# A gated delta net's key-key and query-key products: plain float32 against three terms of exactly split operands

## The chip, the cores and the metric

The kernel runs on one core of a Trainium2 chip. The metric is the device time of one execution in microseconds (us), the median of several runs. Durations inside an execution come from one profiled run of the program.

## The reference, cut to what matters

One layer of a decoder trunk: 512 tokens, a model width of 2048, all in float32. After a norm and one input projection, three groups of heads work side by side: six heads of stick-breaking attention, four groups of a short gated convolution, and six heads of a gated delta net. Their outputs go through an output projection and a squared-ReLU MLP. The change lies in the delta net, of which this is the part that counts:

```python
def gated_delta_rule(q, k, v, g, beta):      # chunks of C tokens, H heads, head width 128
    ...
    k_beta = k * beta[..., None]
    m = jnp.where(strict, jnp.einsum('bhnid,bhnjd->bhnij', k_beta, k) * decay, 0.0)
    t_mat = lax.linalg.triangular_solve(eye + m, ..., lower=True, unit_diagonal=True)
    u = t_mat @ v_beta
    w = t_mat @ (k_beta * jnp.exp(g)[..., None])
    attn_intra = jnp.where(tri, jnp.einsum('bhnid,bhnjd->bhnij', q, k) * decay, 0.0)
    ...
    def step(state, xs):
        v_new = u_c - w_c @ state
        o = q_c @ state + a_c @ v_new
        state = state * jnp.exp(gl_c)[..., None, None] + jnp.swapaxes(k_c, -1, -2) @ v_new
        return state, o
```

`k` and `q` come from the projection through a causal convolution of four taps, a SiLU and an l2 norm. Within a chunk, the products of all keys with all keys (for `m`) and with all queries (for `attn_intra`) are formed, weighted by a decay and masked; a triangular system is solved; then the chunks follow one another through a state.

## The kernel before

Tokens lie along the free dimension (512 columns) and channels along the 128 partitions. The kernel takes chunks of 128 tokens instead of 64, so a head has four blocks (`NB = 4`).

A float32 product can be formed in two ways on TensorE. A matmul with plain float32 operands is one call in the code. Or each operand is split into a high part of type `float32r` and the remainder, also of that type; then three matmuls (high by high, high by low, low by high) are added up in PSUM. The helper `mm3` does this, with one line for each term (L116, L117, L118). The projections (`gemm`, `gemm_chunk`) and the MLP work in this way: ScalarE casts the weights to the high part (`whi`, L103; in the MLP `W`, L841) and VectorE subtracts to get the low part (`wlo`, L104; in the MLP L842). The delta net's own small matmuls are plain float32.

The delta net runs in these steps for each head `h`:

- `gdn_in(h)`: three projections of 48 matmuls x 512 columns (key, query, value; the first head's are computed with the start of the kernel), each through `conv_silu`; `l2n` for key and query. The normalised key and query are written by VectorE into the tile `kq` (L372 and L374), laid out as [128, block, key or query, 128]. Then the value is transposed (L380), the decay matrix is built (L386 to L398: the matmuls are L389), and for each block one matmul takes the key as the stationary operand and key and query together, 256 columns, as the moving operand (L404). VectorE multiplies the two halves of the result with the masked decay into `MT` (L406) and `AT` (L407). PSUM tiles with the tag `i` (two banks) serve the transposition, the decay, the l2 norm and these products in turn.
- `gdn_base(h)`: the triangular inverse, from `MT`. It moves 32x32 blocks through DRAM, runs 31 short steps on VectorE and some small matmuls (L463 to L493).
- `gdn_kdec(h)` and `gdn_scan(h)`: the four blocks in order, each with three to four small matmuls that depend on one another (L507, L512, L517, L526, L530), and at the end a transposition (L544).
- `gdn_gate(h)`: one more projection, the gate.

The calls are written out by hand: `gdn_in(0)`, `base(0)`, `gdn_in(1)`, `scan(0)`, a group of the short convolution, `base(1)`, `gdn_in(2)`, and so on. The order on each engine isn't that of the program text: the framework's planner works out an order for every engine ahead of time from its own costs and from priorities. `base` and `scan` are given a high priority (`CPRIO`), weight loads a medium one (`WPRIO`); `gdn_in` has none. So projections, which need nothing but weights, are placed between the steps of the scans. At run time each engine works through its own order, with semaphores between engines. After the delta net, its SBUF pool (`gdn`) and PSUM pools are closed, and the attention stage opens its own in the same place (`sq`, `sk` and others), starting with the scores (PSUM tag `z`). Then come the output projection and the MLP, which hold most of the time.

Of the kernel before, what the change touches and what calls it, by code (L numbers as in the profile page):

```python
# [11 lines left out]
F32 = mybir.dt.float32  # L12
F32R = mybir.dt.float32r
AF = mybir.ActivationFunctionType
ALU = mybir.AluOpType

P = 128
T = 512
NB = T // P
# [35 lines left out]
def trunk(ctx, tc, xT, wv1, wv2, wa, wo, wu, wd, vec, wf, out, dbg=None):  # L55
    nc = tc.nc
    V, S, G, PE = nc.vector, nc.scalar, nc.gpsimd, nc.tensor
# [19 lines left out]
    def xps(tag):  # L77
        pool, bufs = pool_of[tag]
        return pool.tile([P, 512], F32, name=tag, tag=tag, bufs=bufs)
# [34 lines left out]
    def mm3(p, lh, ll, rh, rl, first, last, more=False):  # L114

        PE.matmul(p, lhsT=lh, rhs=rh, start=first, stop=False, skip_group_check=more)  # L116
        PE.matmul(p, lhsT=lh, rhs=rl, start=False, stop=False, skip_group_check=more)  # L117
        return PE.matmul(p, lhsT=ll, rhs=rh, start=False, stop=last, skip_group_check=more)  # L118
# [10 lines left out]
    def gemm(src, acts):  # L129
        p = mmps()  # L130
        for c in range(KT // CHUNK_KT):
            gemm_chunk(p, src, acts, c)
        return p

    def silu(x, s):

        S.activation(out=s, in_=x, func=AF.Abs)
        S.activation(out=s, in_=s, func=AF.Exp, scale=-1.0)
        S.activation(out=s, in_=s, func=AF.Ln, bias=1.0)
        V.scalar_tensor_tensor(out=s, in0=x, scalar=0.0, in1=s, op0=ALU.min, op1=ALU.subtract)  # L140
        S.activation(out=s, in_=s, func=AF.Exp)
        V.tensor_tensor(out=x, in0=x, in1=s, op=ALU.mult)
# [20 lines left out]
    def col(c):  # L163
        return vc[:, c:c + 1]
# [121 lines left out]
    def ytile(i):  # L286
        return y_pool.tile([P, 512], F32, name="y", tag=f"y{i}", bufs=(10, 6)[i])
# [48 lines left out]
    def gt(shape, name, tag=None, bufs=1, dt=F32):  # L336
        return gp.tile(shape, dt, name=name, tag=tag or name, bufs=bufs)
# [3 lines left out]
    def conv_silu(p, ti):  # L341
        xp = gt([P, 516], "xp", bufs=1)
        G.memset(xp[:, 0:3], 0.0)
        V.tensor_tensor(out=xp[:, 3:515], in0=p, in1=R, op=ALU.mult)
        cv = gt([P, 512], "cv", bufs=2)
        w = lambda i: col(C_GCW + ti * 4 + i)
        S.activation(out=cv, in_=xp[:, 3:515], func=AF.Copy, scale=w(3))
        for i in (2, 1, 0):
            V.scalar_tensor_tensor(out=cv, in0=xp[:, i:i + 512], scalar=w(i), in1=cv, op0=ALU.mult, op1=ALU.add)
        silu(cv, gt([P, 512], "sg", bufs=1))  # L350
        return cv

    def l2n(cv, bias):
        sq = gt([P, 512], "g", tag="g", bufs=4)
        S.activation(out=sq, in_=cv, func=AF.Square)
        hl = [gt([P, 512], "g", tag="g", bufs=4, dt=F32R) for _ in range(2)]
        S.copy(out=hl[0], in_=sq)
        V.tensor_tensor(out=hl[1], in0=sq, in1=hl[0].bitcast(F32), op=ALU.subtract)
        p = xps("i")
        for i in range(2):  # L360
            PE.matmul(p, lhsT=onesR, rhs=hl[i], start=i == 0, stop=i == 1)
        rsqrt_exp(sq, p, 1.0, bias)
        return q4(cv), q4(sq)
# [3 lines left out]
    def gdn_in(h):  # L367
        st = {}
        prod = lambda i: first[i] if h == 0 else gemm(wa[3 * h + i], xw)
        c, r = l2n(conv_silu(prod(0), NH + h), None)  # L370
        kq = gt([P, NB, 2, P], "kq", bufs=3)
        V.tensor_tensor(out=kq[:, :, 0], in0=c, in1=r, op=ALU.mult)  # L372
        c, r = l2n(conv_silu(prod(1), h), lns_c)
        V.tensor_tensor(out=kq[:, :, 1], in0=c, in1=r, op=ALU.mult)  # L374
        cv = conv_silu(prod(2), 2 * NH + h)

        vtok = ytile(1)
        p = xps("i")
        for b in range(NB):
            PE.transpose(p[:, b * P:(b + 1) * P], cv[:, b * P:(b + 1) * P], ident)  # L380
        S.copy(out=vtok, in_=p)

        G1 = [gt([P, NB, P], "g", tag="g", bufs=4, dt=F32R) for i in range(2)]
        for i in range(2):
            for b in range(NB):
                S.activation(out=G1[i][:, b], in_=U32, func=AF.Copy, scale=ghl[:, i, b, h:h + 1].bitcast(F32))  # L386
        p = xps("i")
        for i in range(2):
            PE.matmul(p, lhsT=SLR, rhs=G1[i].rearrange("p b f -> p (b f)"), start=i == 0, stop=i == 1)  # L389
        dti = gt([P, 512], "g", tag="g", bufs=4)  # L390
        dts = gt([P, 512], "g", tag="g", bufs=4)
        S.activation(out=dti, in_=p, func=AF.Exp)
        G.affine_select(out=q4(dts), in_=q4(dti), compare_op=ALU.is_gt, fill=0.0, base=0,
                        pattern=[[0, NB], [1, P]], channel_multiplier=-1)
        G.affine_select(out=q4(dti), in_=q4(dti), compare_op=ALU.is_ge, fill=0.0, base=0,
                        pattern=[[0, NB], [1, P]], channel_multiplier=-1)
        for b in range(NB):
            S.activation(out=q4(dts)[:, b], in_=q4(dts)[:, b], func=AF.Copy, scale=be[:, b, h:h + 1])  # L398
        AT, MT = ytile(1), gt([P, 512], "MT", bufs=3)
        for c in range(2):  # L400
            p = xps("i")
            pv = p.rearrange("p (b w f) -> p b w f", b=2, w=2)
            for b in range(2):
                PE.matmul(pv[:, b], lhsT=kq[:, 2 * c + b, 0], rhs=kq[:, 2 * c + b], start=True, stop=True)  # L404
            s = slice(2 * c, 2 * c + 2)
            V.tensor_tensor(out=q4(MT)[:, s], in0=pv[:, :, 0], in1=q4(dts)[:, s], op=ALU.mult)  # L406
            V.tensor_tensor(out=q4(AT)[:, s], in0=pv[:, :, 1], in1=q4(dti)[:, s], op=ALU.mult)  # L407
        st.update(kq=kq, vtok=vtok, AT=AT, MT=MT)
        heads[h] = st
# [250 lines left out]
    def scan(h):  # L660
        with tc.high_priority(CPRIO):
            gdn_kdec(h)
            gdn_scan(h)

    gdn_in(0)
    base(0)
    gdn_in(1)
    scan(0)
    sc_group(0)
    base(1)  # L670
    gdn_in(2)
    scan(1)
    gdn_gate(0)
# [576 lines left out]
```

## Time and profile before

| what | value |
|---|---|
| runs | 2169.36, 2166.35, 2168.53 us; median 2168.53 |
| the profiled execution | 2170.97 us |
| its span, first to last instruction | 2169.3 us |
| mean granted TensorE clock | 0.996 |
| TensorE matmul (PE) busy | 2140.7 us, 12674 matmuls |
| VectorE (DVE) busy | 1660.4 us |
| ScalarE (ACT) busy | 1073.7 us |
| matmuls of L404 | 48 records |

How to read it: the span is the time between the first and the last instruction in the trace, and the execution's own time is 1.7 us longer. PE is the matmul itself, PEld the load of its stationary operand, which is an instruction of its own. Matmuls are pipelined, so one record can begin before the one ahead of it ends: what a matmul costs is the time from its start to the next one's start, not its recorded duration. Rows of groups read: line, engine, operation, output <- inputs, shapes, count | busy us, mean ns of one | idle time of that engine just before, and what ended it.

### The profile page before, as it was taken

The page shows a single profiled execution, that of the slowest core. Times are in us where ns is not written, and L with a number is a line of the kernel's source. Part 1 is how long each engine was busy: PE and PEld are TensorE (multiplying, and loading weights), DVE is VectorE, ACT ScalarE, POOL GpSimd, SP SyncE. Part 2 cuts the span into 40 slices and gives each one's busy share as a digit, 9 for nine tenths or more (in the row PEclk, how much of TensorE's full clock was granted, in tenths as well). Part 3 has the DMA queues.
Part 4 walks back from the last instruction along what each step waited for, and adds up shares of the span by engine and source line. Part 5 has one row for each costly group of instructions (what it writes and reads, how often), then busy time and mean ns, then how long its engine had stood idle before and what let it go on. Part 6 is the DMA issues. An engine that isn't in the chain of part 4 may idle for free.

```text
span 2169.3 us, 33100 instructions
## 1 busy us (share of the span) xinstructions
PE 2140.7 (99%) x12674; PEld 1884.5 (87%) x12674; DVE 1660.4 (77%) x2360; ACT 1073.7 (49%) x1629; POOL 131.8 (6%) x188
## 2 busy tenths in 40 slices
PE   9999999999999999899999999999999999999998
PEld 8887888888988888799999999999878888888886
DVE  6678978644657755477888788778898898898897
ACT  5646666333445544444444454445544444454455
POOL 0000000000000011100000000000001000000101
PEclk9999999999999999899999999999999999999999
DMA  6333232322222354666666665666896877787674
GB/s 184 107 99 95 82 91 91 92 92 84 83 83 83 103 169 150 215 188 196 194 174 187 195 192 172 191 195 181 280 310 182 242 219 196 208 228 226 184 213 117
DMA packets 160719, 356.42 MB, mean 164 GB/s; under 512 B 20273, under 2 KB 62257, under 8 KB 160433
## 3 DMA queue, kind: packets, MB, share of 16 engines
q1 hardware_dynamic: 146304, 302.93, 41.4%
q0 software_dynamic: 13968, 50.86, 13.6%
q8 instruction: 99, 1.62, 0.3%
q14 instruction: 60, 0.48, 0.1%
q10 hardware_dynamic: 288, 0.52, 0.1%
HBM read 308.90 MB, written 45.36 MB: 163 GB/s over the span
## 4 chain that ended last, share of the span: by engine, by line
PE 92%; DVE 3%; DMA 2%; ACT 1%; issue 1%; SPq 0%; DVEq 0%; ACTq 0%
PE mm L117 10%; PE mm L116 10%; PE mm L118 10%; PE pu L118 10%; PE pu L116 10%; PE pu L117 10%; PE pp L117 9%; PE pp L118 9%; PE pp L116 9%; PE mm L280 1%; PE mm L281 1%; PE mm L279 1%; DMA ha<-hs 1%; DVE W L842 1%; DMA q<-in_wu_dram 0%
## 5 line engine op out<-in xcount | busy, mean ns | idle before, releaser
L841 ACT CAST W<-q 128x1024 fp32r<-128x1024 f32 x446 | 466.7, 1054 | 579.4 <-PE pp L118 258.0
L842 DVE TENSOR_TENSOR W<-q,W 128x1024 fp32r<-128x1024 f32 x446 | 540.9, 1221 | 134.8 <-ACT W L841 130.7
L116 PE MATMUL mm<-big,whi 128*128 128x512 f32 x1024 | 404.8, 396 | 1.3 <-ACT whi L103 0.6
L117 PE MATMUL mm<-big,whi 128*128 128x512 f32 x1024 | 403.9, 394 | 0.0
L118 PE MATMUL mm<-big,wlo 128*128 128x512 f32 x1024 | 402.5, 393 | 0.0
L117 PE MATMUL pp<-W,A 128*128 128x512 f32 x888 | 346.1, 390 | 1.0 <-DVE W L842 1.0
L118 PE MATMUL pp<-W,A 128*128 128x512 f32 x888 | 345.7, 389 | 0.4 <-DVE A L842 0.4
L116 PE MATMUL pp<-W,A 128*128 128x512 f32 x888 | 343.3, 389 | 1.4 <-ACT W L841 1.1
L104 DVE TENSOR_TENSOR wlo<-raw,whi 128x512 fp32r<-128x512 f32 (+1 forms) x292 | 196.6, 675 | 158.3 <-ACT whi L103 150.4
L103 ACT CAST whi<-raw 128x512 fp32r<-128x512 f32 (+1 forms) x292 | 177.3, 608 | 276.5 <-PE mm L117 239.0
L116 PE MATMUL pu<-XS,W 128*128 128x256 f32 x1024 | 288.4, 282 | 9.8 <-ACT W L841 9.6
L118 PE MATMUL pu<-XS,W 128*128 128x256 f32 x1024 | 287.7, 281 | 0.5 <-DVE W L842 0.5
L117 PE MATMUL pu<-XS,W 128*128 128x256 f32 x1024 | 287.8, 281 | 0.0
L116 PEld LDWEIGHTS mm<-big,whi 128*128 128x128 f32 x1024 | 192.4, 188 | 41.4 <-ACT whi L103 2.0
L118 PEld LDWEIGHTS mm<-big,wlo 128*128 128x128 f32 x1024 | 192.4, 188 | 39.1 <-DVE wlo L104 0.3
L117 PEld LDWEIGHTS mm<-big,whi 128*128 128x128 f32 x1024 | 192.5, 188 | 39.0 <-DVE big L734 0.3
L116 PEld LDWEIGHTS pu<-XS,W 128*128 128x128 f32 x1024 | 193.8, 189 | 10.8 <-ACT W L841 9.8
L116 PEld LDWEIGHTS pp<-W,A 128*128 128x128 f32 x888 | 166.7, 188 | 37.1 <-ACT W L841 2.5
L117 PEld LDWEIGHTS pp<-W,A 128*128 128x128 f32 x888 | 166.7, 188 | 37.0 <-DVE W L842 2.5
L118 PEld LDWEIGHTS pp<-W,A 128*128 128x128 f32 x888 | 166.7, 188 | 35.3 <-DVE A L842 0.8
L859 DVE TENSOR_TENSOR q<-q 128x1024 f32<-128x1024 f32 x159 | 193.9, 1220 | 2.2 <-DMA q<-in_wd_dram 0.9
L118 PEld LDWEIGHTS pu<-XS,W 128*128 128x128 f32 x1024 | 193.7, 189 | 0.8 <-DVE W L842 0.8
(302 smaller groups left out, 3284.9 us busy)
## 6 DMA issues: line engine op xcount, KB each, us to landing
q<-in_wu_dram SPq DMA_DIRECT2D x128, 512.0 KB, 4.9
q<-in_wd_dram SPq DMA_DIRECT2D x128, 512.0 KB, 5.6
raw<-in_wa_dram SPq DMA_DIRECT2D x192, 256.0 KB, 2.9
hs<-h SPq DMA_DIRECT2D x32, 1024.0 KB, 5.3
q<-in_wd_dram POOLq DMA_DIRECT2D x64, 512.0 KB, 6.9
ha<-hs SPq DMA_DIRECT2D x55, 512.0 KB, 6.6
q<-in_wu_dram POOLq DMA_DIRECT2D x33, 512.0 KB, 5.6
raw<-in_wo_dram SPq DMA_DIRECT2D x64, 256.0 KB, 3.0
```

What stands on the lines that cost most here:

```text
L103: S.copy(out=hi[:, :n], in_=raw[:, :n])
L104: V.tensor_tensor(out=lo[:, :n], in0=raw[:, :n], in1=hi[:, :n].bitcast(F32), op=ALU.subtract)
L116: PE.matmul(p, lhsT=lh, rhs=rh, start=first, stop=False, skip_group_check=more)
L117: PE.matmul(p, lhsT=lh, rhs=rl, start=False, stop=False, skip_group_check=more)
L118: return PE.matmul(p, lhsT=ll, rhs=rh, start=False, stop=last, skip_group_check=more)
L279: PE.matmul(o, lhsT=xw[k][:, 0, s], rhs=hi[:, ws], start=k == 0 and b % 2 == 0, stop=False)
L280: PE.matmul(o, lhsT=xw[k][:, 0, s], rhs=lo[:, ws], start=False, stop=False)
L281: PE.matmul(o, lhsT=xw[k][:, 1, s], rhs=hi[:, ws], start=False, stop=k == KT - 1 and b % 2 == 1)
L841: return (S.copy(out=o[:, 0], in_=src), V.tensor_tensor(out=o[:, 1], in0=src, in1=o[:, 0].bitcast(F32), op=ALU.subtract))
L842: V.tensor_tensor(out=o[:, 1], in0=src, in1=o[:, 0].bitcast(F32), op=ALU.subtract))
L859: on_v = lambda t, u: V.tensor_tensor(out=t, in0=t, in1=u, op=ALU.add)
```

## The change

In `gdn_in`, the tile `kq` is split into a high and a low part in a new tile `kqs` (one buffer), by a cast on ScalarE and a subtraction on VectorE, each over the whole of the head's keys and queries (128 x 1024). The four products of the head use `mm3` on these parts, three `float32r` matmuls of 256 columns each, instead of one plain float32 matmul. `kq` itself stays, for the scans. All else is left as it was.

```diff
@@ -372,6 +372,9 @@
         V.tensor_tensor(out=kq[:, :, 0], in0=c, in1=r, op=ALU.mult)
         c, r = l2n(conv_silu(prod(1), h), lns_c)
         V.tensor_tensor(out=kq[:, :, 1], in0=c, in1=r, op=ALU.mult)
+        kqs = gt([P, 2, NB, 2, P], "kqs", dt=F32R)
+        S.copy(out=kqs[:, 0], in_=kq)
+        V.tensor_tensor(out=kqs[:, 1], in0=kq, in1=kqs[:, 0].bitcast(F32), op=ALU.subtract)
         cv = conv_silu(prod(2), 2 * NH + h)
 
         vtok = ytile(1)
@@ -400,8 +403,8 @@
         for c in range(2):
             p = xps("i")
             pv = p.rearrange("p (b w f) -> p b w f", b=2, w=2)
-            for b in range(2):
-                PE.matmul(pv[:, b], lhsT=kq[:, 2 * c + b, 0], rhs=kq[:, 2 * c + b], start=True, stop=True)
+            for b in (2 * c, 2 * c + 1):
+                mm3(pv[:, b % 2], kqs[:, 0, b, 0], kqs[:, 1, b, 0], kqs[:, 0, b], kqs[:, 1, b], True, True)
             s = slice(2 * c, 2 * c + 2)
             V.tensor_tensor(out=q4(MT)[:, s], in0=pv[:, :, 0], in1=q4(dts)[:, s], op=ALU.mult)
             V.tensor_tensor(out=q4(AT)[:, s], in0=pv[:, :, 1], in1=q4(dti)[:, s], op=ALU.mult)
```

## The prediction, made before the changed kernel was run

> **What bounds the kernel now.** I read the page's totals and chain first, then the sums by stage, then PE's waits, then the rows of the changed lines. The page:
>
> ```profile
> span 2169.3 us, 33100 instructions
> ...
> PE 2140.7 (99%) x12674; PEld 1884.5 (87%) x12674; DVE 1660.4 (77%) x2360; ACT 1073.7 (49%) x1629; POOL 131.8 (6%) x188
> ...
> PE 92%; DVE 3%; DMA 2%; ACT 1%; issue 1%; SPq 0%; DVEq 0%; ACTq 0%
> ```
>
> PE carries 92% of the chain that ended last, so in most stages a microsecond of matmul saved is a microsecond of kernel. A busy share of 99% alone would not say so, because matmul records overlap. The changed products and the scans that use them lie between about 90 and 530 us. The sums by stage there (busy us of PE, PEld, DVE, ACT, POOL, then clock, DMA share, GB/s):
>
> ```profile
> 60.00:140.00 80.00, 78.99 (x358) 64.73 (x357) 57.24 (x115) 54.05 (x114) 3.43 (x10) 1.00 0.32 98
> 140.00:220.00 80.00, 79.88 (x425) 63.79 (x424) 63.88 (x184) 42.67 (x89) 3.70 (x10) 1.00 0.34 98
> 220.00:300.00 80.00, 80.00 (x428) 65.35 (x427) 70.80 (x190) 53.86 (x112) 2.23 (x7) 1.00 0.29 89
> 300.00:380.00 80.00, 80.00 (x434) 65.31 (x433) 62.95 (x167) 48.89 (x105) 3.19 (x9) 1.00 0.29 87
> ```
>
> PE has next to no idle time there (at most 1.0 of 80 us), at a granted clock of 1.00. VectorE is the next engine (70.80 of 80 us at its fullest), ScalarE has a third or more free. PE's waits from 60 to 560 us (total, times, longest):
>
> ```profile
> PE r L226 <- ACT R L146: 0.8, 1, 0.8
> PE z L116 <- ACT sk L582: 0.4, 1, 0.4
> PE mm L116 <- ACT sq L585: 0.4, 1, 0.4
> PE mm L116 <- DVE xp L344: 0.2, 1, 0.2
> ```
>
> None is in the delta net's own work: its latencies are covered by projection matmuls (mm) that stand between its steps in PE's order. The feed of those projections runs ahead:
>
> ```profile
> L103 ACT CAST whi<-raw 128x512 fp32r<-128x512 f32 x152 | 94.0, 619 | 129.3 <-PE mm L117 115.8 <-PE mm L281 6.4 <-DVE Yq L449 2.4
> ```
>
> ScalarE's idle time ahead of the weight casts was ended by PE in 115.8 of 129.3 us: the casts wait for PE to free a buffer, not PE for the casts.
>
> **The change part by part.** *The products.* Each head has four products (one for each block of 128 tokens) of 256 columns, six heads 24. Their rows now:
>
> ```profile
> L404 PEld LDWEIGHTS i<-kq x48: 186/189/192, 111.5 to 378.5; 128*128 128x128 f32 x48
> L404 PE MATMUL i<-kq x48: 377/379/483, 111.7 to 378.7; 128*128 128x256 f32 x48
> L507 PE MATMUL s<-Sn,kq x36: 270/275/377, 198.9 to 508.1; 128*128 128x128 f32 x36
> L372 DVE TENSOR_TENSOR kq<-cv,g x6: 680/685/694, 90.1 to 354.7; 128x512 f32<-128x512 f32 x6
> L374 DVE TENSOR_TENSOR kq<-cv,g x6: 682/685/689, 96.6 to 355.3; 128x512 f32<-128x512 f32 x6
> ```
>
> 48 matmuls for 24 products: a plain float32 product is issued as two passes. The recorded 379 ns is a latency; what a pass costs is start to start. The first head:
>
> ```profile
> 111.45 0.40 PE L118 MATMUL mm<-big,wlo 128*128 128x512 f32 x1
> 111.68 1.02 PE L404 MATMUL i<-kq 128*128 128x256 f32 x4
> 112.36 0.58 PE L116 MATMUL mm<-big,whi 128*128 128x512 f32 x1
> 112.78 1.02 PE L404 MATMUL i<-kq 128*128 128x256 f32 x4
> 113.45 0.58 PE L117 MATMUL mm<-big,whi 128*128 128x512 f32 x1
> 113.87 0.39 PE L118 MATMUL mm<-big,wlo 128*128 128x512 f32 x1
> 114.10 0.39 PE L116 MATMUL mm<-big,whi 128*128 128x512 f32 x1
> ```
>
> From 111.68 to 113.87 are 2.19 us for eight passes and two projection matmuls; one of the latter takes 0.23 (113.87 to 114.10, also 111.45 to 111.68). So eight passes take 2.19 - 0.46 = 1.73, a pass 0.216 and a product 0.432 us. The new form has three float32r matmuls of 128x128 by 256 columns. The MLP runs that very form; the first and the last of 27 in a row:
>
> ```profile
> 999.83 0.28 PE L116 MATMUL pu<-XS,W 128*128 128x256 f32 x1
> ...
> 1002.88 0.28 PE L118 MATMUL pu<-XS,W 128*128 128x256 f32 x1
> ```
>
> 26 steps in 3.05 us: 0.117 each, three 0.352. A product saves 0.080 us, 24 save 1.9 us, all on PE in a stage that PE bounds. PE also gets 24 more matmuls and 24 more weight loads (72 of each for 48). The row of L404 has 483 ns at most against a median of 379, which I read as the price of a load that isn't hidden: 0.104 us. Bounds for the 72 loads: none exposed, 0; all exposed, 72 x 0.104 = 7.5 us. I take none, the value of the stretch of 27, which is the same form with as many loads per matmul.
>
> The Trainium skill, "TensorE: Matmul & The Clock Gate", Part 3, speaks against that: a weight load overlaps running matmuls only where the row group differs, and here every load fills all rows. Put as rows of this kernel, each load would add its own 189 ns: 3 x (0.117 + 0.189) = 0.918 against 2 x (0.216 + 0.189) = 0.810 a product, 24 x 0.108 = 2.6 us lost instead of 1.9 gained. The 27 matmuls disagree: loads of about 0.19 us fit into steps of 0.117, which a load that stood alone could not. It stays a small rival.
>
> *The split.* Per head one ScalarE cast and one VectorE subtraction over 128x1024, the forms of the MLP's weight split:
>
> ```profile
> L841 ACT CAST W<-q 128x1024 fp32r<-128x1024 f32 x446 | 466.7, 1054 | 579.4 <-PE pp L118 258.0
> L842 DVE TENSOR_TENSOR W<-q,W 128x1024 fp32r<-128x1024 f32 x446 | 540.9, 1221 | 134.8 <-ACT W L841 130.7
> ```
>
> 1.05 us of ScalarE and 1.22 us of VectorE a head, 6.3 and 7.3 us in all, spread over some 290 us. VectorE at 70.80 of 80 would rise to about 73. I cost both at nothing: PE's other work covers them. Without that cover, the latency is 1.05 + 1.22 = 2.28 us a head. The new wait (first product behind the subtraction, behind the cast, behind L374) holds up, on in-order VectorE, whatever stands behind the subtraction: weight splits (L104) and the third convolution of the head (L349). And on PE, all projections behind the product. The cover is the time from the last write of kq to the first product. Head 0: 96.6 + 0.7 = 97.3 to 111.7, 14.4 us. The tightest I found is head 2:
>
> ```profile
> L404 PE MATMUL i<-kq x8: 379/379/483, 202.0 to 204.7; 128*128 128x256 f32 x8
> ...
> L374 DVE TENSOR_TENSOR kq<-cv,g x1: 683/683/683, 191.8 to 191.8; 128x512 f32<-128x512 f32 x1
> ```
>
> 192.5 to 202.0, 9.5 us, four times the split. Bounds: fully covered 0; never covered 6 x 2.28 = 13.7 us. I take 0, as the products have other work ahead of them: transposing v (L380), the decay matrix (L389), PSUM banks of the tag i.
>
> *The end of the stage.* The scans run one after another from 198.9 to 508.1 us (L507 above), and the attention stage starts behind the last:
>
> ```profile
> 526.73 0.60 PE L544 MATMUL o<-ident,MT 128*128 128x128 f32 x4
> ...
> 528.31 0.40 PE L118 MATMUL mm<-big,wlo 128*128 128x512 f32 x1
> 529.06 0.79 PE L116 MATMUL z<-sk,sq 128*128 128x512 f32 x3 [0.36 <-ACT sk L582]
> ...
> 530.95 0.28 PE L118 MATMUL z<-sk,sq 128*128 128x256 f32 x1
> 531.58 0.50 PE L116 MATMUL mm<-big,whi 128*128 128x512 f32 x1 [0.35 <-ACT sq L585]
> ```
>
> Here the projections that can run ahead are used up: PE loses 529.06 - 528.31 - 0.23 = 0.5 us, and 531.58 - 530.95 - 0.12 = 0.5 more. If the scans ended later against PE's work, this gap would grow. Head 0's split could push the row of scans back by 2.28 us at most; its 14.4 us of cover say 0. The new tile kqs (8 KB a partition, one buffer) is last read by the sixth head's products at about 379 us, 148 us ahead of the tiles that take its place: 0.
>
> *Sum.* -1.9 + 0 + 0. The profiled execution took 2170.97 us by its own time (span 2169.3), 2.4 above the median of 2168.53; it would become 2169.1, and the median 2166.6 us. That is 0.09%, below the 0.2% (4.3 us) that a measurement of this kernel can tell from no change.
>
> **The rivals.** *Slower: PE stands at the products.* All engines run in an order fixed by the framework's planner. If it puts the products nearer to the subtraction, PE waits for the split, and the projections behind it wait too. For it: VectorE at 70.80 of 80 in the stage of head 3. Against it: 9.5 us and more of cover. At 2.28 us a head it outweighs the saving from one head on; three heads give 6.8 - 1.9 = +4.9, 2173.4 us, which decides for slower by over 0.2%; six give 2180.3.
>
> *Loads exposed.* From 18 of the 72 (1.9 / 0.104) the saving is gone, all 72 give 7.5 - 1.9 = +5.6, 2174.1 us; by the 189 ns of a load on both sides 2171.1. For it: the 483 ns of L404. Against it: the 27 in a row.
>
> *The scans end later.* Head 0's split moves the row of scans, PE's saving only widens the gap at 528.5: +2.3, 2170.8 us. No change that can be told.
>
> *Faster: another order.* New durations make the planner lay the stage out anew. Between 60 and 560 us the projections' matmuls are recorded longer than the late stage's:
>
> ```profile
> L117 PE MATMUL mm<-big,whi 128*128 128x512 f32 x586 | 232.8, 397 | 0.0
> L116 PE MATMUL mm<-big,whi 128*128 128x512 f32 x586 | 232.3, 396 | 0.6 <-ACT sq L585 0.4 <-DVE xp L344 0.2
> L118 PE MATMUL mm<-big,wlo 128*128 128x512 f32 x586 | 231.7, 395 | 0.0
> ...
> L117 PE MATMUL pp<-W,A 128*128 128x512 f32 x888 | 346.1, 390 | 1.0 <-DVE W L842 1.0
> ```
>
> That is 586 x (7 + 6 + 5) ns = 10.5 us of short stalls around the small matmuls. A third of them and the saving give -3.5 - 1.9 = -5.4, 2163.1 us. Against it: nothing in the change aims there, and an order can get worse too.
>
> **How the numbers follow.** Forecast 2166.6: 0.44. PE at the products: 0.18, of which 0.16 above 4.3 us. Loads exposed: 0.06, half of it above. Scans later: 0.10. Another order, faster: 0.22. So faster 0.22; same 0.44 + 0.02 + 0.03 + 0.10 = 0.59; slower 0.19. The range runs from 2161.5 (half of the short stalls and the saving, -5.3 - 1.9 = -7.2) to 2175.5 (between three and four heads waiting, 9.0 - 1.9 = +7.1): it takes in the rivals' times and leaves out the tail of six heads.
>
> **What the profile after would show.** Right: the products as 72 matmuls about 0.117 us apart, 0.70 instead of 0.86 us for a pair; no wait of PE on kqs; ScalarE and VectorE up by 6.3 and 7.3 us; span down by about 2 us. Wrong: PE waits on kqs; steps of 0.22 between the new matmuls; a gap ahead of the first z matmul well over 0.5 us; or a difference that lies behind 560 us, where nothing is changed.

## The result and the profile after

The changed kernel takes 2170.88 us (median of 20 runs, 2168.84 to 2174.38) against 2168.00 for the kernel before on the same chip: a ratio of 1.0015 [1.0009, 1.0021]. It is 2.9 us slower; forecast were 1.9 us less. A later set of 11 runs gave 2170.97 and 1.0016 [1.0008, 1.0025].

The page of the changed kernel: PE is busy 4.5 us less, VectorE 9.0 and ScalarE 5.6 us more, and the span stays (2169.2 for 2169.3 us). The profiled execution of before, with 2170.97 us, lies above all 20 runs of that kernel (2165.92 to 2169.46), so the two spans are a poor comparison.

```profile
span 2169.2 us, 33163 instructions
...
PE 2136.2 (98%) x12698; PEld 1882.6 (87%) x12698; DVE 1669.4 (77%) x2366; ACT 1079.3 (50%) x1635; POOL 133.1 (6%) x188
```

A better mark is the point where all projections, scans and scores are done, the first transposition of the output projection (tile `t`). The group of these matmuls in before and then in after; the time after "first and last start" is the mark:

```profile
L774 PE MATMUL t<-ident,x x60: 270/272/328, 746.7 to 889.5; 128*128 128x128 f32 x60
```

```profile
L777 PE MATMUL t<-ident,x x60: 270/272/327, 749.3 to 892.1; 128*128 128x128 f32 x60
```

Up to there after is 2.6 us behind, close to the 2.9 of the medians. Behind the mark PE's matmuls and their order are the same in both; there before's profiled execution took 2169.3 - 746.7 = 1422.6 us and after's 2169.2 - 749.3 = 1419.9, which hides the loss in the spans. So the loss lies before 749 us. A mark is that of one execution: a second one of after has it at 748.2, only 1.5 us behind before. The sums by stage of after (columns as in the prediction):

```profile
140.00:180.00 40.00, 37.83 (x198) 29.96 (x197) 34.20 (x104) 18.32 (x35) 2.09 (x5) 1.00 0.35 102
...
220.00:300.00 80.00, 80.00 (x430) 65.24 (x429) 71.20 (x182) 53.16 (x109) 2.96 (x7) 1.00 0.28 86
...
460.00:500.00 40.00, 37.05 (x178) 30.29 (x177) 21.04 (x37) 12.74 (x27) 0.10 (x1) 1.00 0.27 86
500.00:540.00 40.00, 40.00 (x188) 33.28 (x187) 16.09 (x27) 14.24 (x30) 0.88 (x3) 1.00 0.29 89
```

and of before in the same stages:

```profile
140.00:180.00 40.00, 39.88 (x208) 31.69 (x207) 33.69 (x103) 17.12 (x34) 1.77 (x5) 1.00 0.34 98
460.00:500.00 40.00, 39.87 (x192) 33.10 (x190) 21.89 (x37) 13.78 (x28) 0.10 (x1) 1.00 0.31 99
500.00:540.00 40.00, 39.24 (x182) 32.08 (x181) 17.39 (x29) 13.38 (x28) 1.90 (x4) 1.00 0.26 81
```

PE's idle time is 40 minus the second number. It grows by 2.05 us at 140 to 180 (2.17 for 0.12) and by 2.82 us at 460 to 500 (2.95 for 0.13), and falls by 0.76 us at 500 to 540: +4.1. With 1.9 us of saved product time that leaves +2.2 of the +2.6 us. In the stage where VectorE is fullest (220 to 300) PE loses nothing. What PE waits for in after, 60 to 560 us:

```profile
PE s L520 <- ACT vn L517: 1.7, 2, 1.0
PE i L361 <- ACT g L357: 1.2, 1, 1.2
PE b L466 <- DMA X<-sy: 1.0, 1, 1.0
PE r L226 <- ACT R L146: 0.8, 1, 0.8
PE mm L116 <- DVE tmp L567: 0.6, 1, 0.6
PE s L510 <- ACT Sn L523: 0.4, 1, 0.4
PE o L529 <- ACT y L549: 0.3, 1, 0.3
PE mm L116 <- DVE xp L344: 0.2, 1, 0.2
```

No line has `kqs`: PE never waits for the split at the products. The new waits are for other work. The wait on `X`, the block that the triangular inverse brings back from DRAM, ends at 160.7 us, and that on L357, in the l2 norm, at 169.7. Those on `vn`, `Sn` and `y` belong to the scans' own chain, which in before had projections ahead of every step. Their place in after's timeline of PE:

```profile
480.13 0.40 PE L118 MATMUL mm<-big,wlo 128*128 128x512 f32 x1
480.37 0.38 PE L515 MATMUL s<-y,MT 128*128 128x128 f32 x2
481.50 0.49 PE L520 MATMUL s<-vn,kdec 128*128 128x128 f32 x2 [0.75 <-ACT vn L517]
482.35 0.49 PE L510 MATMUL s<-Sn,kq 128*128 128x128 f32 x2 [0.35 <-ACT Sn L523]
482.67 0.60 PE L547 MATMUL o<-ident,MT 128*128 128x128 f32 x4
...
484.05 0.49 PE L529 MATMUL o<-vn,y 128*128 128x128 f32 x2 [0.28 <-ACT y L549]
485.53 0.49 PE L520 MATMUL s<-vn,kdec 128*128 128x128 f32 x2 [0.99 <-ACT vn L517]
...
486.22 0.48 PE L116 MATMUL mm<-big,whi 128*128 128x512 f32 x1
```

Between 480.13 and 486.22 us there is no projection matmul: the last step of the fifth scan and the first steps of the sixth stand back to back, and PE waits between them. The transposition that ends the fifth scan (`o<-ident`) starts at 482.67; in before it started at 469.03, with the sixth scan's steps 5 to 7 us apart and projections between them:

```profile
469.03 0.66 PE L544 MATMUL o<-ident,MT 128*128 128x128 f32 x4
...
475.95 0.38 PE L507 MATMUL s<-Sn,kq 128*128 128x128 f32 x2
...
482.35 0.38 PE L512 MATMUL s<-bp,MT 128*128 128x128 f32 x2
...
487.62 0.38 PE L517 MATMUL s<-vn,kdec 128*128 128x128 f32 x2
```

Two theories fit this. *Work*: the split's own time on VectorE, set among the steps of the triangular inverse, makes the scans late. *Order*: the planner has laid out all engines anew from the first head's value convolution on, and that order would lose the time whatever the split takes. A third, that the new products cost more than forecast, is tested first. In the expectations below, theory A is *work*, theory B is *order* and theory C is the products.

### The profile page after: what moved, and what is told of

It is laid out like the page before. It is cut to its first block, busy times and chain, and to the rows that moved or that the text cites. A ratio compares the mean times of both kernels' runs of the same rounds, so it can differ in the third digit from the quotient of the medians.

```text
span 2169.2 us, 33163 instructions
## 1 busy us (share of the span) xinstructions
PE 2136.2 (98%) x12698; PEld 1882.6 (87%) x12698; DVE 1669.4 (77%) x2366; ACT 1079.3 (50%) x1635; POOL 133.1 (6%) x188
## 3 DMA queue, kind: packets, MB, share of 16 engines
q8 instruction: 99, 1.62, 0.3%
## 4 chain that ended last, share of the span: by engine, by line
PE 94%; DVE 2%; DMA 1%; ACT 1%; issue 1%; SPq 0%; DVEq 0%; ACTq 0%
PE mm L116 11%; PE mm L118 10%; PE mm L117 10%; PE pu L118 10%; PE pu L116 10%; PE pu L117 10%; PE pp L117 9%; PE pp L118 9%; PE pp L116 9%; PE mm L280 1%; PE mm L281 1%; PE mm L279 1%; DMA q<-in_wu_dram 0%; DVE W L845 0%; DMA q<-in_wd_dram 0%
```

## The experiments

Each ratio is against runs of the kernel before on the same chip, with its 95% interval. "The mark" is the first start of the `t` group in the profiled execution.

**The products alone.** `products_only`: `kq` is written as `float32r`, the low part is a tile of zeros, and there is no split; it leaves out the low part of keys and queries, but none of the matmuls.

```diff
-        kq = gt([P, NB, 2, P], "kq", bufs=3)
+        kr = gt([P, NB, 2, P], "kq", bufs=3, dt=F32R)
+        kq = kr.bitcast(F32)
...
-                PE.matmul(pv[:, b], lhsT=kq[:, 2 * c + b, 0], rhs=kq[:, 2 * c + b], start=True, stop=True)
+                mm3(pv[:, b % 2], kr[:, b, 0], klo[:, 0], kr[:, b], klo, True, True)
```

> The changed kernel without the split: the key and query are written as float32r by the same two VectorE instructions, the low part is a tile of zeros, and the products are the same three matmuls. It leaves out the low parts, so keys and queries are rounded. Theory A: the VectorE time is gone and the saving on PE stays, so 1.9 us below the kernel before (-1 to -3), the scans end as early as before. Theory B: anything from -5 to +5 us. Theory C: slower than before by 2 to 4 us, as the changed kernel.

Measured: 2165.43 against 2167.69 us, 0.9987 [0.9978, 0.9996]: 2.3 us less, where the prediction's term is 1.9. The products aren't the loss. (This kernel, too, has an order of its own by the planner. In its profile the fifth scan ends at 475.16 us, 6.1 later than in before, where theory A had expected no delay, and PE waits 1.4 us on `X`, without any split. So a late scan alone is no loss: it costs where no projections stand between its steps in PE's order.)

**The split alone.** `split_only`: before with the cast and the subtraction added, their result unused.

```diff
+        kqs = gt([P, 2, NB, 2, P], "kqs", dt=F32R)
+        S.copy(out=kqs[:, 0], in_=kq)
+        V.tensor_tensor(out=kqs[:, 1], in0=kq, in1=kqs[:, 0].bitcast(F32), op=ALU.subtract)
```

> Kernel before plus the split alone: the cast and the subtraction of each head are made, and nothing reads their result; the products stay plain float32. Theory A (the subtraction's 1.22 us of VectorE a head falls among the 62 VectorE steps of the head before, the scans end later and the projections between them run out): slower than before by what the change lost plus its 1.9 us of saving, some +3 to +6 us, with the end of the first triangular inverse at 187 us or later (before 182.8) and PE idle about 480 us. Theory B (the planner lays any changed program out anew, the loss is chance and has nothing to do with VectorE): anything from -5 to +5 us, and no tie between the ends of the scans and the time. Theory C (the new products cost more on PE than the rows say): no change, within 1 us.

Measured: 2172.82 us, 1.0026 [1.0015, 1.0036]: 5.1 us more. So the loss comes with these two lines. Both signs that the expectation names for theory A are there: the last matmuls of the first inverse start at 187.10 us (182.38 in before), and PE stands idle for 1.62 us up to 484.51. But the two lines also make the planner lay out a new order, so this doesn't yet tell work from order.

**The split off VectorE.** `split_on_pool`: the changed kernel with the subtraction on GpSimd.

```diff
-        V.tensor_tensor(out=kqs[:, 1], in0=kq, in1=kqs[:, 0].bitcast(F32), op=ALU.subtract)
+        G.tensor_tensor(out=kqs[:, 1], in0=kq, in1=kqs[:, 0].bitcast(F32), op=ALU.subtract)
```

> The changed kernel with the subtraction on GpSimd instead of VectorE; it computes the same. A 128x512 addition takes 1.36 us there, so some 2.7 us a head, against 9.5 us and more of time between the key and the products. Theory A: VectorE is as free as before and the saving on PE stays: -1 to -3 us against before. Theory B: anything from -5 to +5 us. Theory C: as the changed kernel, +2 to +4 us.

Measured: 2172.32 us, 1.0018 [1.0009, 1.0027]. The loss stays, but this run doesn't free VectorE. GpSimd needs 2.70 us for one subtraction (median of six), and beside each of the six one step of VectorE is stretched to 2.3 to 2.5 us. Head 1's, beside a step of the inverse that took 0.26 us in before:

```profile
135.49 2.87 POOL L377 TENSOR_TENSOR kqs<-kq,kqs 128x1024 fp32r<-128x1024 f32 x1 [4.17 <-ACT kqs L376]
...
136.18 2.29 DVE L452 TENSOR_TENSOR Yq<-Yq,tq 128x92 f32<-128x92 f32 x1
```

VectorE is busy for 1673.1 us in all, more than with the subtraction on it (1669.4). So the expectation's premise, a VectorE as free as before, does not hold, the order is again a new one, and the run decides nothing between work and order.

**A new order from nearly no work.** `tiny_op`: before with a copy of 128x4 on VectorE in each head, its result unused.

```diff
+        dead = gt([P, 4], "dead")
+        V.tensor_copy(out=dead, in_=kq[:, 0, 0, 0:4])
```

> Kernel before plus one VectorE copy of 128x4 for each head, that nothing reads, in the place of the split: some 0.1 to 0.2 us of VectorE a head, but a changed program for the planner. Theory A: within 1 us of before. Theory B: a move of 2 us or more either way, with ends of the scans that differ from before by several us.

Measured: 2171.05 us, 1.0012 [1.0003, 1.0021]: 3.4 us more for six copies of four columns. PE's waits, 60 to 560 us, have a new one on `tmp` at 480 us, and the one of the first scores on `sk` is 1.7 us for before's 0.4:

```profile
PE z L116 <- ACT sk L584: 1.7, 1, 1.7
PE mm L116 <- DVE tmp L570: 1.1, 1, 1.1
```

The operation is too small to matter by its work, and in the planner's new order there are waits that before does not have. The third scan ends 3.1 us later than in before and the fifth 7.1, the others within 1.1. This kernel's own mark, 747.2, is only 0.5 us behind before's, so its profiled execution shows less than its runs do; by its runs the order theory gains, though nothing here holds the work fixed.

**The change in the order of before.** `after_pinned`: the changed kernel, but every engine's instructions are queued in the order of before, by edges that set the order and add no semaphore. The three matmuls of a product stand where the one stood; casts and subtractions are put at written places, head 1's subtraction at about 136 us.

```diff
+        for a, b in zip(order, order[1:]):                          # for each engine
+            tc.add_manual_dep(b, a.name, info, reason="pin")        # info: no semaphore
```

> The changed kernel, with every engine held to the order of the kernel before: the six casts and the six subtractions are put into gaps that ScalarE and VectorE had there, and the three matmuls of a product stand where its two passes stood. Order theory (the loss is the new order that the planner made): -1.9 us against before for the products, up to 1.2 given back because the second head's subtraction finds no gap among the steps of the first head's inverse and PE waits there for the block that comes back from DRAM; so -0.5 to -2.5 us. Work theory (the split's VectorE time costs by itself, whatever the order): +2 us or more, as the changed kernel. Product theory (the new matmuls are dearer than their rows): +2 us or more.

Measured: 2166.49 us against 2167.34, 0.9994 [0.9985, 1.0003]. The same work is 4.4 us faster than in the planner's order, and the mark is 744.2, 5.1 us ahead of after and 2.5 ahead of before:

```profile
L785 PE MATMUL t<-ident,x x60: 270/272/327, 744.2 to 887.0; 128*128 128x128 f32 x60
```

Its fifth scan ends 2.5 us earlier than before's, and of after's new waits only the one on `X` is left:

```profile
466.50 0.65 PE L555 MATMUL o<-ident,MT 128*128 128x128 f32 x4
```

```profile
PE b L474 <- DMA X<-sy: 0.8, 2, 0.6
```

**The control.** `before_pinned`: before with the same edges, to see what the pinning itself does.

> The kernel before with its own order written out: a control for the pinning itself, and a second profile of before. All theories: within 1 us of before.

Measured: 2167.60 us, 1.0002 [0.9992, 1.0011]; nothing.

**The split's own price.** `split_pinned`: before with the unused split, in before's order and at the same places.

> The split alone, its result read by nothing, in the order of the kernel before on every engine. Order theory: 0 to +1.3 us, all of it one wait of PE at about 159 us for the first head's block from DRAM. Work theory: +3 to +5 us, as the split alone was under the planner's order (+5.1).

Measured: 2169.06 us, 1.0005 [0.9996, 1.0014], mark 748.1. PE has one new wait, of 1.8 us:

```profile
PE b L472 <- DMA X<-sy: 1.8, 2, 1.5
```

Head 1's subtraction stands on VectorE among the 62 instructions (31 steps of two) of head 0's triangular inverse; the block that goes through DRAM comes later, and PE waits, which in before it did not. So the work may have a price too: 1.5 us against the pinned before by the medians, about a third of what the order costs (below). The interval doesn't tell it from nothing, and reaches up to 3 us. `after_pinned` differs from this kernel in the products alone, and is 2.6 us faster by the medians, while its wait for `X` is 1.0 us shorter: the products save time in one and the same order too.

**That subtraction on GpSimd.** `after_pinned_pool1`: `after_pinned` with head 1's subtraction alone moved.

> As the changed kernel in the order of before, but the second head's subtraction runs on GpSimd (2.7 us there), which is idle at that time, so that the first head's inverse isn't held up on VectorE. Order theory: -1.9 us (-1 to -3). If it comes out level with the pinned changed kernel, the wait for the first head's block doesn't count.

Measured: 2167.77 us, 1.0000 [0.9992, 1.0009]. The expected gain did not come: by the medians this is 1.3 us more than `after_pinned`, and the wait for `X` did not go; it was 1.7 us in one piece. The trace shows why `X` is late there too. While GpSimd subtracts, one step of the inverse on VectorE, of 0.21 us in before, takes 2.42 us:

```profile
140.34 2.83 POOL L383 TENSOR_TENSOR kqs<-kq,kqs 128x1024 fp32r<-128x1024 f32 x1
...
140.84 2.42 DVE L460 TENSOR_TENSOR Yq<-Yq,tq 128x60 f32<-128x60 f32 x1
```

That is 2.2 us lost in one step, more than the 1.22 us that the move saves on VectorE.

**The order of after with the work of before.** `before_after_order`: the same edges, now with after's order, on the kernel before (no split, plain products). It completes the square of two kinds of work and two orders.

> The work of before (plain products, no split), queued on every engine in the order of after. The order theory: the order costs by itself what separates after from its twin in before's order, 4.4 us, so this kernel goes to about 2171.9 us (2170 to 2173), 4 us above before, with the scans ending some 8 to 14 us later than in before (the fifth near 480 us instead of 469) and PE waits near 159 and 480 us. The rival, that the order only hurts together with the split's time on VectorE: 2167 to 2168.5 us, no scan more than 4 us late, first scores at 529 to 530 us.

Measured: 2172.58 us, 1.0020 [1.0011, 1.0029], 5.1 us more than before for the same work. Its timeline of PE shows after's waits at the scans, at the same steps and of the same length, without a split in the kernel:

```profile
478.98 0.38 PE L518 MATMUL s<-y,MT 128*128 128x128 f32 x2
480.12 0.49 PE L523 MATMUL s<-vn,kdec 128*128 128x128 f32 x2 [0.75 <-ACT vn L520]
480.96 0.49 PE L513 MATMUL s<-Sn,kq 128*128 128x128 f32 x2 [0.35 <-ACT Sn L526]
481.29 0.60 PE L550 MATMUL o<-ident,MT 128*128 128x128 f32 x4
...
482.66 0.49 PE L532 MATMUL o<-vn,y 128*128 128x128 f32 x2 [0.28 <-ACT y L552]
484.14 0.62 PE L523 MATMUL s<-vn,kdec 128*128 128x128 f32 x2 [0.99 <-ACT vn L520]
```

0.75, 0.35, 0.28 and 0.99 us, as in after, and the fifth scan ends at 481.29 for 469.03. The first scores start at 532.9 us (532.7 in after, 529.1 in before). Its 140 to 180 us have no idle time, though, where the expectation had a wait near 159: in after's order the wait on L357 is there only with the split, and that on `X` in one of two executions with it.

```profile
140.00:180.00 40.00, 40.00 (x209) 31.84 (x208) 34.86 (x104) 19.89 (x37) 1.77 (x5) 1.00 0.35 103
...
460.00:500.00 40.00, 37.05 (x171) 30.30 (x170) 21.23 (x37) 12.45 (x27) 0.10 (x1) 0.96 0.25 80
```

Its mark is 749.5, 2.8 us behind before's. The other 2.3 us of the difference between the medians have no place in this trace that can be shown; its profiled execution, with 2175.24 us, was the longest of its 11 runs.

**The changed kernel again**, `after_again`, beside the one above on the same chip.

> The changed kernel as it is, beside the two others. Both theories: 2170.9 us within 1.5, some 4 us above its twin in before's order; the first scores near 532.7 us and the output projection near 749.3 us, as in its first profile.

Measured: 2170.97 us, 1.0016 [1.0008, 1.0025]; its profile has the first scores at 531.6 and the mark at 748.2, each 1.1 us earlier than expected, with the same waits at 480 us.

| median, us | order of before | order of after |
|---|---|---|
| work of before | 2167.47; pinned 2167.60 | 2172.58 |
| work of after | 2166.49 | 2170.97 |

Down a column (the work) the change gains 1.1 and 1.6 us; along a row (the order) it loses 5.0 and 4.5 us. In the first row the interval against before is [1.0011, 1.0029], and in the second the two intervals, [0.9985, 1.0003] and [1.0008, 1.0025], don't overlap: the order's cost is clear of the noise. The gains down a column are not, each for itself. The pinned kernels in before's order and the two in after's order come from two sets of runs; before's own median differs by 0.13 us between these.

**The wait for `X` moved.** `after_pinned_later`: `after_pinned` with head 0's first group of 32x32 matmuls, which waits for `X`, put behind six more projection matmuls on PE.

```diff
- ... mm, [b<-X x8], mm, mm, mm, mm, mm, mm, ...      # PE's written order, head 0
+ ... mm, mm, mm, mm, mm, mm, mm, [b<-X x8], ...
```

> The changed kernel in before's order, with head 0's first group of 32x32 matmuls (it waits for the block from DRAM that the subtraction made late) put behind six more projection matmuls on PE, 1.4 us of work. If that wait (0.64 + 0.20 us in the twin's profile, at 156 to 157 us) is what the split still costs there, it goes, and the time falls by about 0.8 us from 2166.5 to 2165.7; the scans end within 0.5 us of the twin's. If instead the scans' row sets the time, the 0.3 us by which the group comes later is passed on and the time stays at 2166.5 to 2167.

Measured: 2166.00 us, 0.9993 [0.9983, 1.0002]; against its twin's 0.9994 no difference. The time lies between the two forecasts, 2165.7 and 2166.5 to 2167, and doesn't tell them apart; the trace does. The wait on `X` is gone and one of the same size stands at the chain's next step:

```profile
158.45 0.66 PE L474 MATMUL b<-X,MT 32*32 32x32 f32 x16
...
165.02 0.44 PE L483 MATMUL b<-Xc,A 32*32 32x32 f32 x16 [0.89 <-DVE A L478]
```

The wait was passed on, as the second half of the expectation had it: the whole chain is late, not one step of it. It is the fastest version with the full computation, but not told apart from before.

## Why the prediction was wrong, point by point

- *The products*, -1.9 us: right. Twelve of them in after's timeline of PE take 1.43 us from 111.55 to 112.98, 0.119 each (forecast 0.117). `products_only` gained 2.3 us, and in one and the same order the kernel with them was 2.6 us faster (`after_pinned` against `split_pinned`).

```profile
111.55 0.28 PE L116 MATMUL i<-kqs 128*128 128x256 f32 x1
...
112.98 0.40 PE L116 MATMUL mm<-big,whi 128*128 128x512 f32 x1
```

- *Loads exposed*: did not happen. In after the loads of these matmuls take 186 to 192 ns and the steps 119, so they overlap the matmuls ahead of them although all fill every row. The rule of the Trainium skill ("TensorE: Matmul & The Clock Gate", Part 3), by which they would not, doesn't hold for this kernel.

```profile
L118 PEld LDWEIGHTS i<-kqs x24: 186/192/192, 111.7 to 390.2; 128*128 128x128 f32 x24
...
L376 ACT CAST kqs<-kq x6: 1035/1040/1057, 97.1 to 367.7; 128x1024 fp32r<-128x1024 f32 x6
L377 DVE TENSOR_TENSOR kqs<-kq,kqs x6: 1182/1219/1227, 98.2 to 369.3; 128x1024 fp32r<-128x1024 f32 x6
```

- *The split*: its size was right (6 x 1.04 and 6 x 1.22 us), and so was the cover of the products (no wait on `kqs`). "I cost both at nothing" was not quite. I asked who waits for the subtraction's result, and of what stands behind it on VectorE I named only weight splits and a convolution. Head 1's stands among the steps of head 0's triangular inverse. In before's order the price was a wait of 0.8 us (`after_pinned`) to 1.8 us (`split_pinned`).
- *The end of the stage*, "its 14.4 us of cover say 0": the step that failed, by most. I measured the covers in before's order and took that order as given, so the sum "-1.9 + 0 + 0" has no term for a new one. The runs showed 5.0 us for the order alone with before's work and 4.5 us with after's. In after the scans end late, the fifth by 14 us though the sixth by only 1, for a reason that has no duration in it: the planner's new order. The place was wrong too. I had in mind the gap ahead of the first scores (528 us); there after has no idle time left (40.00 of 40 for 39.24). What the profile can place was paid mainly at 480 to 486 us, with 2.4 us of idle time, and at 160 to 170 us, with 2.2.
- *The rivals*: "PE stands at the products" fell. "The scans end later" gave 2170.8 us, a tenth from what was measured, but by another mechanism (head 0's split, the gap at 528 us), so the number agrees by luck. "Another order" was the mechanism, and I entered it as a gain only, with one clause that an order can get worse. Orders laid out by the planner after an edit gave 2165.4 (`products_only`), 2170.9, 2171.1, 2172.3 and 2172.8 us, each with its work: a spread of 7.4 us, almost four times the saving, and four of the five above before's 2167.7.
- *The signs*: what was named as right came, but for the span (VectorE and ScalarE rose by 9.0 and 5.6 us for 7.3 and 6.3), and none of the signs named as wrong points at the loss. The list had none for a new order.
- *The sums*: small slips change nothing. A change of -7.2 leads to 2161.3, not 2161.5, and ScalarE has 32% free in two of the four stages, not a third or more. The 0.2% that a measurement could tell was too coarse: with 20 runs of each kernel the interval is 0.06% to each side, and 0.15% stands out.

Why the planner prefers the order that it chose is open; no run shows its costs.

## What to carry over

Where a planner lays out the engines, an edit's price is its work plus a new order, and here the order was 4.5 to 5 us against 1.1 to 1.6 us of gain: put both orders on both kinds of work before explaining a difference of this size, and give a new order chances on both sides in a forecast. When costing an added instruction on an in-order engine, list whose chain it is set into, not only who waits for its result. Moving an operation to another engine frees the first one only if its other steps keep their length: compare them in the trace. Here, removing one wait of a late chain moved it to the chain's next step.

## What the runs showed of the hardware

A short wait of PE can be followed by a stretch at half its clock. In `split_pinned` the wait for `X` (1.54 us in the timeline, then 0.8 us with only 32x32 matmuls) was followed by projection matmuls 0.43 us apart instead of 0.23. The granted clock is the third number from the end:

```profile
158.00:160.00 2.00, 1.50 (x19) 1.14 (x20) 1.42 (x5) 0.00 (x0) 0.00 (x0) 0.83 0.10 36
160.00:162.00 2.00, 2.00 (x6) 1.61 (x5) 2.00 (x5) 1.49 (x3) 0.00 (x0) 0.50 0.00 0
```

The slow steps start at 159.11 and end at 162.54, 3.4 us: eight steps of 0.43 us where 0.23 is usual, so an estimated 1.6 us lost. `before_after_order` has it behind its scan waits, where `after_again` with the same waits keeps a clock of 1.00:

```profile
484.00:486.00 2.00, 1.86 (x8) 1.76 (x9) 2.00 (x5) 1.23 (x4) 0.00 (x0) 0.59 0.11 20
486.00:488.00 2.00, 2.00 (x7) 1.57 (x6) 2.00 (x5) 0.00 (x0) 0.00 (x0) 0.56 0.69 227
```

`split_on_pool` and `split_only` both wait 1.74 us ahead of the first scores; behind it the first has 0.54 from 536 to 538 us and the second 1.00. So the same wait costs the clock in some executions only, and what decides it no run shows.

How much of the order's cost is paid this way is not shown either. Of the first 20 executions of the changed kernel, nine with a mean granted clock of 0.996 average 2169.8 us, five with 0.995 average 2171.0, and six with 0.994 average 2172.9; all 26 runs of before beside the last set have 0.995 or 0.996. But a mean does not say where the clock was lost. Behind PE's wait of 9 to 10 us at the start of the MLP it is at half in every profiled execution, in some longer than in others (0.50 from 908 to 912 us in before). The execution of `split_only` with 0.994 has 1.00 from 60 to 890 us, and is slow at the start of the MLP and again at 1594. Neither profiled execution of the changed kernel has a slow stretch between 60 and 900 us.

The Trainium skill ("TensorE: Matmul & The Clock Gate", Part 1) describes a clock halved after an idle window of about 3.4 us, with windows that run freely. The half clock and the 3.4 us agree; that a single wait of half that length can be enough, it doesn't say.

GpSimd and VectorE are not independent: beside a GpSimd subtraction of 2.4 to 3.1 us a VectorE step took 2.3 to 2.5 us in all six heads of `split_on_pool`, where the same operations took 0.16 to 0.75 us in before.
